# An encoder layer with three mixers: weight tiles split once and fetched as two parts, and an FFN input normalised ahead of its products

## The chip, the cores and the metric

The kernel runs on one core of a Trainium2 chip. The metric is the device time in microseconds of one execution of the whole program; the runs are compared by their median. Engine names are those of the profile: PE (TensorE matmul), PEld (its weight loads), DVE (VectorE), ACT (ScalarE), POOL (GpSimd), SP (SyncE, which here issues every DMA).

## The reference

One encoder layer over 2048 tokens of width 1024, in fp32:

```
h = rms_norm(x) * norm_mix;  p = h @ w_in          # 13 parts of p feed three mixers
out_a = sparse attention: an indexer scores all keys, each query keeps its 256 best, softmax over them
out_b = gated linear attention in chunks of 64;  out_c = sliding window attention with sinks
x = x + concat(out_a, out_b, out_c) @ w_out
h = rms_norm(x) * norm_ffn
x = x + (silu(h @ w_ffn_gate) * (h @ w_ffn_up)) @ w_ffn_down      # inner width 2816
return rms_norm(x) * final_norm
```

## The kernel before

**Layout.** Activations are kept transposed: a tile has 128 channels on the partitions and 512 tokens along the free side. The 2048 tokens are four groups of 512 (NG, G), the 1024 channels eight chunks (KC), the inner width 22 chunks (NF).

**Split products.** A product in fp32 is made of three matmuls in fp32r, of 512 columns each. Every operand is split in a part hi, rounded to fp32r, and a remainder lo. `split` (L113) does that with a cast on ACT (L116) and a subtraction on POOL (L119), and `product` (L150) and `proj` (L469) issue hi x hi, lo x hi and hi x lo for each chunk.

**Weights.** A weight tile is 128 x 512, which is four chunks of 128 x 128, 256 KB. Each use of a tile begins with `load_w` (L142 in the FFN, L459 in the projections): SP fetches it from DRAM to one of three buffers `raw`, and `split` fills a slot of `whi` and one of `wlo`. There are three such slots in the projections (A_W), five in the FFN of groups 0 and 1 (N_W), nine in the last FFN. The same tile of w_in is used for each of the four groups; the tiles of w_out and of the three FFN matrices are used three times, once for group 0, once for group 1 and once for groups 2 and 3 together, and each time fetched and split anew.

**Two threads.** `dense` (L1073) does `pass1` for the four groups (the parts of p that the sparse attention needs), then `pass2` (gated linear and window attention), then `ffn` for groups 0 and 1. `dsa` (L1058) does the sparse attention for 16 blocks of 128 queries: `select` (L825) searches the threshold of the 256 best by 31 halvings, each a count over all keys (on ACT at L888, on DVE at L890 in turn) and two DVE steps of one column (L913 and L915), while `attend` (L953) works on the block before. `merge` (L43) interleaves the two threads by the costs that they yield. A planner then puts the instructions in order for each engine: of those that it takes for ready, the earliest in the program goes first, and each engine runs its own in that order. An `ffn` begins with the attention's result for its groups (mixT in DRAM). When both threads are done, `ffn` runs for groups 2 and 3 (two halves of 512 tokens) by itself.

**The FFN** (L135). `mixed` (L186) fetches the mixers' output and splits it. For each output chunk oc and each half the w_out product is made, first over chunks 2 to 7 (`others`), then over 0 and 1 (`sparse`), which come from the sparse attention and are late; the first n_lead products go ahead without them. `residual` (L194) adds x and sums the squares. Then h2, x2 times the norm's weight but not yet times 1/rms, is split (L230, L231). For each f, `gate_up` (L234) makes the gate and the up product for each half; the factor 1/rms, `rs`, comes from a matmul with ones after the first gate product (`norm_scale`, L178), and is multiplied in behind the products:

```
V.tensor_mul(z, pg, rs[:, hs])       # L247: gate, from PSUM
Q.tensor_mul(u, z, rs[:, hs])        # L249
sigmoid(z, s)                        # L128 to L132: Abs, Exp, Ln, a DVE step, Exp
V.tensor_mul(u, pu, u)               # L254: up, from PSUM
Q.tensor_mul(u, u, s)                # L255
split(u, ah[:, hs], al[:, hs])
```

`down` (L259) multiplies two chunks f at a time by w_down and adds to x2 (L274). The last `down` also sums squares, and `finish` (L290) scales and stores the output. The sigmoid is written with Exp and Ln, as the norms are (`rstd_of`, L121), and one table is loaded on ACT at the start (L90).

Of the kernel before, what the change touches and what calls it, by code (L numbers as in the profile page):

```python
# [8 lines left out]
F32 = mybir.dt.float32  # L9
# [10 lines left out]
P = 128  # L20
# [64 lines left out]
def hybrid_encoder_kernel(ctx, tc, xT, w_in, w_out, w_g, w_u, w_d, vec, wuk, wuv, wg2,  # L85
# [27 lines left out]
    def split(src, hi, lo, hi_eng=None):  # L113
# [21 lines left out]
    def ffn(groups, pools, ps_f, ps_n, n_raw, n_w, n_act, n_lead, before):  # L135
# [3 lines left out]
        W = nh * 512  # L139
        halves = [slice(i * 512, (i + 1) * 512) for i in range(nh)]  # L140

        def load_w(src):  # L142
            raw = fr.tile([P, 512], F32, tag="raw", bufs=n_raw, name="raw")
            nc.sync.dma_start(out=raw, in_=src)
            hi = fh.tile([P, 512], F32R, tag="whi", bufs=n_w, name="whi")
            lo = fl.tile([P, 512], F32R, tag="wlo", bufs=n_w, name="wlo")
            split(raw, hi, lo)
            return hi, lo

        def product(ps, w, act, hs, ks=range(KC), first=True, last=True):  # L150
            for k in ks:
                hi, lo = w[k // 4]
                a, b = (t[:, (k % 4) * P:(k % 4 + 1) * P] for t in (hi, lo))
                T.matmul(ps, a, act[k][0][:, hs], start=(first and k == ks[0]), stop=False)  # L154
                T.matmul(ps, b, act[k][0][:, hs], start=False, stop=False)  # L155
                T.matmul(ps, a, act[k][1][:, hs], start=False, stop=(last and k == ks[-1]))  # L156
# [6 lines left out]
        def operand(k):  # L163
            pool = fo if k in others else fs
            return (pool.tile([P, W], F32R, tag=f"ah{k}", bufs=1, name="ah"),
                    pool.tile([P, W], F32R, tag=f"al{k}", bufs=1, name="al"))

        def square(hs, k):

# [11 lines left out]
            T.matmul(pm, ones, rs[:, hs], start=True, stop=True)  # L181
            rstd_of(pm, D, rs[:, hs])

        mixo = [operand(k) for k in range(KC)]

        def mixed(k):  # L186
            for g, hs in zip(groups, halves):
                hi, lo = (t[:, hs] for t in mixo[k])
                m = fr.tile([P, 512], F32, tag="m", bufs=3, name="m")
                nc.sync.dma_start(out=m, in_=mixT[g][k])  # L190
                A.copy(hi, m)
                (V if k % 2 else Q).tensor_sub(lo, m, hi.bitcast(F32))  # L192

        def residual(oc, i, ps):  # L194
            g, hs = groups[i], halves[i]
# [1 line left out]
            V.tensor_add(x2[:, oc, hs], x2[:, oc, hs], ps)  # L197
            square(hs, oc)

        for k in others:  # L200
            mixed(k)
            yield 0.5
        lead = []
        for oc in range(KC):
            w = [load_w(w_out[oc][:, i * 512:(i + 1) * 512]) for i in range(2)]
            for i, hs in enumerate(halves):
                ps = ps_f()
                yield from product(ps, w, mixo, hs, others, last=False)
                lead.append((oc, i, ps, w, hs))
                yield 3.9 - 0.65 * (KC - FINE)  # L210
                if oc * nh + i < n_lead - 1:
                    continue
                if oc * nh + i == n_lead - 1:
                    yield from before
                    rs = fx.tile([P, W], F32, tag="rs", bufs=1, name="rs")
                    x2 = fx.tile([P, KC, W], F32, tag="x2", bufs=1, name="x2")
                    for k in sparse:
                        mixed(k)
                while lead:
                    oc_, i_, ps, w_, hs_ = lead.pop(0)  # L220
                    yield from product(ps, w_, mixo, hs_, sparse, first=False)
                    residual(oc_, i_, ps)
                    yield 1.3

        h2 = [operand(k) for k in range(KC)]
        for hs in halves:
            for k in range(KC):
                gk = vc[:, V_FFN + k:V_FFN + k + 1]
                hi, lo = h2[k][0][:, hs], h2[k][1][:, hs]
                A.activation(hi, x2[:, k, hs], AF.Copy, scale=gk)  # L230
                V.scalar_tensor_tensor(out=lo, in0=x2[:, k, hs], scalar=gk, in1=hi.bitcast(F32),  # L231
                                       op0=ALU.mult, op1=ALU.subtract)

        def gate_up(f):  # L234
            ah = ft.tile([P, W], F32R, tag="fh", bufs=n_act, name="fh")
            al = ft.tile([P, W], F32R, tag="fl", bufs=n_act, name="fl")
            wg_ = [load_w(w_g[f][:, i * 512:(i + 1) * 512]) for i in range(2)]
            wu_ = [load_w(w_u[f][:, i * 512:(i + 1) * 512]) for i in range(2)]
            acts[f] = (ah, al)
            for i, hs in enumerate(halves):  # L240
                pg = ps_f()
                yield from product(pg, wg_, h2, hs)
                if f == 0:
                    norm_scale(hs)
                s = ft.tile([P, 512], F32, tag="s", bufs=2, name="s")
                z = ft.tile([P, 512], F32, tag="z", bufs=2, name="z")
                V.tensor_mul(z, pg, rs[:, hs])  # L247
                u = ft.tile([P, 512], F32, tag="u", bufs=2, name="u")
                Q.tensor_mul(u, z, rs[:, hs])  # L249
                sigmoid(z, s)  # L250
                yield 5.2 - 0.65 * (KC - FINE)
                pu = ps_f()
                yield from product(pu, wu_, h2, hs)
                V.tensor_mul(u, pu, u)  # L254
                Q.tensor_mul(u, u, s)  # L255
                split(u, ah[:, hs], al[:, hs])
                yield 5.2 - 0.65 * (KC - FINE)

        def down(fs, parts, last=False):  # L259

            n, ws = len(fs), {}
            for i2, hs in parts:
                if i2 not in ws:
                    ws[i2] = [load_w(w_d[f][:, i2 * 512:(i2 + 1) * 512]) for f in fs]
# [58 lines left out]
    with ExitStack() as mx:  # L323
# [132 lines left out]
                yield 0.4  # L456
            return hh, hl

        def load_w(src):  # L459
            raw = wp.tile([P, 512], F32, tag="raw", bufs=A_RAW, name="raw")  # L460
            nc.sync.dma_start(out=raw, in_=src)
            hi = wp.tile([P, 512], F32R, tag="whi", name="whi")
            lo = wp.tile([P, 512], F32R, tag="wlo", name="wlo")
            split(raw, hi, lo)
            return hi, lo

        PART = 0.65 * (KC - FINE)

        def proj(c, h, ws=()):  # L469
# [2 lines left out]
            ps = ps_mm()  # L472
            for k in range(KC):
                if k % 4 == 0:
                    hi, lo = ws[k // 4] if ws else load_w(w_in[c][:, k * P:k * P + 512])
# [7 lines left out]


        def pass1(g):
            ws = [load_w(w_in[CH_C][:, i * 512:(i + 1) * 512]) for i in range(2)]
            h, acc = yield from scaled_in(g)
            g0 = g * G

# [709 lines left out]
```

## Time and profile before

| | us |
|---|---|
| runs: median (lowest to highest) | 3005.09 (3005.06 to 3010.59) |
| the profiled execution: time | 3006.77 |
| the profiled execution: span in the trace | 3005.0 |
| PE / DVE / ACT / POOL busy | 2773.4 / 1803.9 / 1556.9 / 1372.3 |

The trace has one execution. Busy time of PE is to be read with care: matmuls overlap, each is shown as some 390 ns, and one can start every 226 ns. A share of busy time over the whole span is a mean over stages that differ; so the views below are cut by stage.

### The profile page before, as it was taken

The numbers are of one execution on the slowest core, as the hardware profiler recorded it, in microseconds if no ns is written. First come the engines' busy times: TensorE is split into PE (matmuls) and PEld (weight loads), VectorE is DVE, ScalarE is ACT, GpSimd is POOL, SyncE is SP. The second block draws the span as 40 slices with busy tenths as digits, with TensorE's granted clock in tenths as the row PEclk, the third lists the DMA queues.
The fourth block names the chain that finished last, engine by engine and source line by source line (L and its number), as shares of the span: only waits on it lengthen the run. The fifth ranks groups of instructions, "written<-read, shape, count | busy, mean of one in ns | idle before, by whom it ended". The sixth has DMA issues, their size and how long they took to land.

```text
span 3005.0 us, 38463 instructions
## 1 busy us (share of the span) xinstructions
PE 2773.4 (92%) x13364; PEld 2177.9 (72%) x13364; DVE 1803.9 (60%) x3638; ACT 1556.9 (52%) x2734; POOL 1372.3 (46%) x1085
## 2 busy tenths in 40 slices
PE   7688989999999989999989989999799999999997
PEld 5466757666676767777767777777588888888886
DVE  4588788786877867667577476575423223332226
ACT  4566666566565756565475464565525333223333
POOL 4334323333233345655654556546425445444543
PEclk9889999999999999999999999999999999999998
DMA  5444222122222322222223222222421111111111
GB/s 158 124 123 131 75 66 90 61 92 66 60 68 71 114 81 77 85 78 74 83 90 134 76 73 82 76 71 74 136 98 50 50 46 53 49 48 44 53 46 56
DMA packets 158874, 239.07 MB, mean 80 GB/s; under 512 B 16248, under 2 KB 56472, under 8 KB 158680
## 3 DMA queue, kind: packets, MB, share of 16 engines
q1 hardware_dynamic: 158680, 236.62, 25.2%
q8 instruction: 105, 1.72, 0.2%
q14 instruction: 89, 0.73, 0.1%
HBM read 212.83 MB, written 23.72 MB: 79 GB/s over the span
## 4 chain that ended last, share of the span: by engine, by line
PE 44%; DVE 10%; issue 5%; ACT 5%; POOL 4%; DMA 1%; DVEq 0%; SPq 0%; POOLq 0%; ACTq 0%
PE pf L154 6%; PE pf L156 6%; PE pf L155 6%; DVE jd L890 4%; PE mf L154 3%; PE mf L156 3%; PE mf L155 3%; PE pf L273 3%; PE pf L271 3%; PE pf L272 3%; POOL wlo L119 2%; ACT jd L888 2%; PE mf L271 2%; PE mf L273 2%; PE mf L272 1%
## 5 line engine op out<-in xcount | busy, mean ns | idle before, releaser
L119 POOL TENSOR_TENSOR wlo<-raw,whi 128x512 fp32r<-128x512 f32 x620 | 841.0, 1364 | 999.7 <-ACT whi L116 928.2
L116 ACT CAST whi<-raw 128x512 fp32r<-128x512 f32 x620 | 377.8, 616 | 420.7 <-PE pf L273 142.9
L888 ACT ACTIVATE jd<-x,c 128x384 bf16<-128x384 f32 (+13 forms) x224 | 292.6, 1306 | 191.1 <-DVE c L915 146.0
L154 PE MATMUL mf<-ah,whi 128*128 128x512 f32 x832 | 331.3, 398 | 13.3 <-ACT ah L230 10.9
L477 PE MATMUL mm<-hh,whi 128*128 128x512 f32 x704 | 297.9, 424 | 40.8 <-ACT hh L432 32.7
L890 DVE TENSOR_SCALAR_CACHE_REDUCE jd<-x,c 128x384 bf16<-128x384 f32 (+13 forms) x224 | 331.0, 1478 | 6.9
L156 PE MATMUL mf<-al,whi 128*128 128x512 f32 x832 | 327.9, 395 | 6.5 <-POOL al L192 3.5
L155 PE MATMUL mf<-ah,wlo 128*128 128x512 f32 x832 | 327.8, 395 | 0.9 <-POOL wlo L119 0.9
L154 PE MATMUL pf<-ah,whi 128*128 128x512 f32 x832 | 324.6, 390 | 1.0 <-issue 1.0
L155 PE MATMUL pf<-ah,wlo 128*128 128x512 f32 x832 | 323.7, 389 | 0.0
L156 PE MATMUL pf<-al,whi 128*128 128x512 f32 x832 | 323.6, 389 | 0.0
L479 PE MATMUL mm<-hl,whi 128*128 128x512 f32 x704 | 287.7, 412 | 7.1 <-DVE hl L433 6.0
L478 PE MATMUL mm<-hh,wlo 128*128 128x512 f32 x704 | 288.0, 410 | 2.7 <-POOL wlo L119 2.7
L477 PEld LDWEIGHTS mm<-hh,whi 128*128 128x128 f32 x704 | 138.4, 197 | 86.0 <-ACT hh L432 34.7
L154 PEld LDWEIGHTS mf<-ah,whi 128*128 128x128 f32 x832 | 158.2, 190 | 48.5 <-ACT ah L230 11.4
L156 PEld LDWEIGHTS mf<-al,whi 128*128 128x128 f32 x832 | 157.9, 190 | 41.8 <-POOL al L192 4.3
L274 DVE TENSOR_TENSOR x<-x,pf 128x512 f32<-128x512 f32 (+1 forms) x184 | 121.8, 664 | 109.4 <-PE pf L273 109.1
L155 PEld LDWEIGHTS mf<-ah,wlo 128*128 128x128 f32 x832 | 158.2, 190 | 34.2 <-POOL wlo L119 1.9
L271 PE MATMUL mf<-fh,whi 128*128 128x512 f32 x352 | 145.5, 413 | 39.8 <-DVE u L254 27.6
L154 PEld LDWEIGHTS pf<-ah,whi 128*128 128x128 f32 x832 | 156.2, 188 | 33.9 <-issue 1.5
L155 PEld LDWEIGHTS pf<-ah,wlo 128*128 128x128 f32 x832 | 156.2, 188 | 32.9 <-issue 0.5
L156 PEld LDWEIGHTS pf<-al,whi 128*128 128x128 f32 x832 | 156.1, 188 | 32.7 <-DVE al L231 0.2
(246 smaller groups left out, 5740.2 us busy)
## 6 DMA issues: line engine op xcount, KB each, us to landing
raw<-in_w_in_dram SPq DMA_DIRECT2D x176, 256.0 KB, 2.7
raw<-in_w_g_dram SPq DMA_DIRECT2D x132, 256.0 KB, 2.6
raw<-in_w_u_dram SPq DMA_DIRECT2D x132, 256.0 KB, 2.7
raw<-in_w_d_dram SPq DMA_DIRECT2D x132, 256.0 KB, 2.7
xk<-in_xT_dram SPq DMA_DIRECT2D x64, 256.0 KB, 2.9
raw<-in_w_out_dram SPq DMA_DIRECT2D x48, 256.0 KB, 3.0
m<-mixT SPq DMA_DIRECT2D x32, 256.0 KB, 3.3
x<-in_xT_dram SPq DMA_DIRECT2D x32, 256.0 KB, 4.5
```

The costliest lines, as they stand in the source:

```text
L116: A.copy(hi, src)
L119: Q.tensor_sub(lo, src, hi.bitcast(F32))
L154: T.matmul(ps, a, act[k][0][:, hs], start=(first and k == ks[0]), stop=False)
L155: T.matmul(ps, b, act[k][0][:, hs], start=False, stop=False)
L156: T.matmul(ps, a, act[k][1][:, hs], start=False, stop=(last and k == ks[-1]))
L271: T.matmul(ps, hi[:, os_], ah[:, hs], start=(j == 0), stop=False)
L273: T.matmul(ps, hi[:, os_], al[:, hs], start=False, stop=(j == n - 1))
L477: T.matmul(ps, a, hh[k], start=(k == 0), stop=False)
L478: T.matmul(ps, b, hh[k], start=False, stop=False)
L479: T.matmul(ps, a, hl[k], start=False, stop=(k == KC - 1))
L888: A.activation(jd, xs, AF.Sign, scale=-1.0, bias=c[:, 0:1], accum_out=cnt)
L890: V.tensor_scalar(out=jd, in0=xs, scalar1=c[:, 0:1], scalar2=0.0, op0=ALU.is_ge, op1=ALU.add, accum_out=cnt)
```

## The change

The change does three things.

1. `load_halves` and `store_halves` are new. A slot `w` has both parts of a weight tile, 128 x 1024. At the first use of a tile it is fetched and split as before and, two loads later, stored to DRAM in both parts (512 KB). At each later use both parts come from there with one DMA, straight to the slot, without `raw` and `split`. The numbers of slots and of raw buffers stay.
2. The FFN takes one half after the other in the w_out products (so the last FFN runs through w_out twice), fetches the second half's mixT tiles during the first half's last products, and `normed` makes h2 with 1/rms in it, per half, before the gate and up products.
3. The gate is pg * (1 + tanh(pg / 2)) / 2: one Tanh that reads PSUM, and two fused DVE steps, the second with the up product.

The diff, cut to its core (`mixed`, `operand` and `product` now take a half's own tiles instead of a slice; `proj`'s `load_w` calls `load_halves` in the same way with slots of `wp`):

```diff
+    halved, unstored = {}, []
+    def load_halves(key, src, raw_pool, n_raw, pool, n_w):
+        w = pool.tile([P, 1024], F32R, tag="w", bufs=n_w, name="w")
+        hi, lo = w[:, 0:512], w[:, 512:1024]
+        if key in halved:
+            while unstored:
+                store_halves()
+            nc.sync.dma_start(out=w.bitcast(F32), in_=halved[key])
+            return hi, lo
+        raw = raw_pool.tile([P, 512], F32, tag="raw", bufs=n_raw, name="raw")
+        nc.sync.dma_start(out=raw, in_=src)
+        split(raw, hi, lo)
+        halved[key] = dram.tile([P, 1024], F32, name=f"w{len(halved)}")
+        unstored.append((halved[key], w))
+        if len(unstored) > 2:
+            store_halves()
+        return hi, lo
+    def store_halves():
+        dst, w = unstored.pop(0)
+        nc.sync.dma_start(out=dst, in_=w.bitcast(F32))
...
-        def load_w(src):
...
+        def load_w(src, f, c):
+            return load_halves((src.tensor.name, f, c), src[f][:, c * 512:(c + 1) * 512], fr, n_raw, fh, n_w)
...
+        def normed(i):
+            hs = halves[i]
+            norm_scale(hs)
+            h2.append([])
+            for k in range(KC):
+                h2[i].append(operand(i, k))
+                hi, lo = h2[i][k]
+                hf = fr.tile([P, 512], F32, tag="m", bufs=3, name="hf")
+                V.scalar_tensor_tensor(out=hf, in0=x2[:, k, hs], scalar=vc[:, V_FFN + k:V_FFN + k + 1],
+                                       in1=rs[:, hs], op0=ALU.mult, op1=ALU.mult)
+                A.copy(hi, hf)
+                (V if k % 2 else Q).tensor_sub(lo, hf, hi.bitcast(F32))
+                yield 0.4
...
-        for oc in range(KC):
-            w = [load_w(w_out[oc][:, i * 512:(i + 1) * 512]) for i in range(2)]
-            for i, hs in enumerate(halves):
+        for i, hs in enumerate(halves):
+            lead = []
+            for oc in range(KC):
+                w = [load_w(w_out, oc, c) for c in range(2)]
...
+                if i + 1 < nh and oc >= n_lead:
+                    for k in range((oc - n_lead) * KC // (KC - n_lead), (oc + 1 - n_lead) * KC // (KC - n_lead)):
+                        mixed(i + 1, k)
...
-        h2 = [operand(k) for k in range(KC)]
-        for hs in halves:
-            for k in range(KC):
-                gk = vc[:, V_FFN + k:V_FFN + k + 1]
-                hi, lo = h2[k][0][:, hs], h2[k][1][:, hs]
-                A.activation(hi, x2[:, k, hs], AF.Copy, scale=gk)
-                V.scalar_tensor_tensor(out=lo, in0=x2[:, k, hs], scalar=gk, in1=hi.bitcast(F32),
-                                       op0=ALU.mult, op1=ALU.subtract)
+            yield from normed(i)
...
                 pg = ps_f()
-                yield from product(pg, wg_, h2, hs)
-                if f == 0:
-                    norm_scale(hs)
+                yield from product(pg, wg_, h2[i])
                 s = ft.tile([P, 512], F32, tag="s", bufs=2, name="s")
-                z = ft.tile([P, 512], F32, tag="z", bufs=2, name="z")
-                V.tensor_mul(z, pg, rs[:, hs])
-                u = ft.tile([P, 512], F32, tag="u", bufs=2, name="u")
-                Q.tensor_mul(u, z, rs[:, hs])
-                sigmoid(z, s)
+                A.activation(s, pg, AF.Tanh, scale=0.5)
+                V.scalar_tensor_tensor(out=s, in0=s, scalar=1.0, in1=pg, op0=ALU.add, op1=ALU.mult)
...
-                V.tensor_mul(u, pu, u)
-                Q.tensor_mul(u, u, s)
+                u = ft.tile([P, 512], F32, tag="u", bufs=2, name="u")
+                V.scalar_tensor_tensor(out=u, in0=s, scalar=0.5, in1=pu, op0=ALU.mult, op1=ALU.mult)
                 split(u, ah[:, hs], al[:, hs])
...
+            while unstored:
+                store_halves()
             dx.close()
```

## Rows read from the trace of the kernel before

**Rows 1.** Page, section 1: engine, busy us (share of the span), instructions.
```profile
PE 2773.4 (92%) x13364; PEld 2177.9 (72%) x13364; DVE 1803.9 (60%) x3638; ACT 1556.9 (52%) x2734; POOL 1372.3 (46%) x1085
```

**Rows 2.** Stages: window, length, busy us (instructions) per engine, granted clock, DMA share, GB/s.
```profile
0.00:1034.00 1034.00, 914.25 (x4607) 669.46 (x4608) 774.40 (x1925) 629.97 (x1268) 364.33 (x316) 0.94 0.30 91
1034.00:1572.00 538.00, 501.12 (x2455) 401.55 (x2454) 367.99 (x669) 319.30 (x506) 303.96 (x234) 0.98 0.27 84
1572.00:2120.00 548.00, 505.32 (x2425) 404.76 (x2424) 354.37 (x593) 306.03 (x467) 305.65 (x228) 0.97 0.25 82
2120.00:2176.00 56.00, 40.83 (x273) 29.75 (x272) 27.86 (x59) 32.33 (x53) 27.10 (x21) 0.88 0.50 163
2176.00:2960.00 784.00, 784.00 (x3456) 648.25 (x3455) 244.59 (x339) 246.57 (x398) 354.06 (x272) 1.00 0.16 53
```

**Rows 3.** The same view, 100 us in the middle of the last stage.
```profile
2300.00:2400.00 100.00, 100.00 (x443) 82.81 (x442) 27.08 (x37) 34.55 (x56) 53.87 (x42) 1.00 0.17 53
```

**Rows 4.** Groups: tile, shape, count | busy us, mean ns | idle before, releasers.
```profile
L119 POOL TENSOR_TENSOR wlo<-raw,whi 128x512 fp32r<-128x512 f32 x620 | 841.0, 1364 | 999.7 <-ACT whi L116 928.2 <-issue 46.7 <-PE mm L478 7.0
L116 ACT CAST whi<-raw 128x512 fp32r<-128x512 f32 x620 | 377.8, 616 | 420.7 <-PE pf L273 142.9 <-PE pf L156 92.7 <-PE mf L156 71.2
L154 PE MATMUL mf<-ah,whi 128*128 128x512 f32 x832 | 331.3, 398 | 13.3 <-ACT ah L230 10.9 <-DVE x L274 1.3 <-ACT ah L191 0.9
...
L478 PE MATMUL mm<-hh,wlo 128*128 128x512 f32 x704 | 288.0, 410 | 2.7 <-POOL wlo L119 2.7
...
L271 PE MATMUL mf<-fh,whi 128*128 128x512 f32 x352 | 145.5, 413 | 39.8 <-DVE u L254 27.6 <-DVE x L274 10.3 <-ACT fh L116 1.7
...
L249 POOL TENSOR_TENSOR u<-z,rs 128x512 f32<-128x512 f32 x88 | 122.5, 1393 | 59.6 <-DVE z L247 56.3 <-DMA raw<-in_w_d_dram 2.3 <-DVE e L904 1.0
...
L255 POOL TENSOR_TENSOR u<-u,s 128x512 f32<-128x512 f32 x88 | 116.8, 1327 | 121.7 <-DVE u L254 101.9 <-ACT s L132 13.0 <-ACT whi L116 6.9
...
L130 ACT ACTIVATE s<-s 128x512 f32<-128x512 f32 x88 | 55.6, 631 | 2.1
...
L231 DVE SCALAR_TENSOR_TENSOR al<-x,vc,ah 128x512 fp32r<-128x512 f32 x32 | 24.9, 828 | 0.6 <-ACT ah L230 0.5
...
L230 ACT ACTIVATE ah<-x,vc 128x512 fp32r<-128x512 f32 x32 | 20.8, 711 | 4.5 <-PE pf L155 4.5
```

**Rows 5.** Chain of waits, shares of the window: 1034 to 1572, then 1572 to 2120.
```profile
by line: issue 13.5%; DVE jd L890 9.2%; PE mf L154 7.8%; PE mf L155 7.4%; PE mf L156 7.4%; ACT jd L888 5.2%; POOL wlo L119 4.5%; PE mf L271 4.2%; PE mf L273 4.1%; PE mf L272 4.0%; PE o L1011 2.1%; POOL u L255 1.6%; DVE up L913 1.6%; ACT big
...
by line: issue 14.3%; DVE jd L890 11.0%; PE mf L156 7.2%; PE mf L154 7.2%; PE mf L155 7.1%; POOL wlo L119 5.4%; PE mf L271 4.5%; PE mf L273 4.3%; PE mf L272 4.2%; ACT jd L888 4.2%; POOL u L255 2.2%; PE o L1011 1.7%; DVE up L913 1.6%; DVE c 
```

**Rows 6.** Stages, the instructions of line 119 alone.
```profile
0.00:1034.00 1034.00, 260.57 (x191) 0.94 0.30 91
```

**Rows 7.** DMA issues: count, KB each, median us from issue to landing.
```profile
raw<-in_w_in_dram SPq DMA_DIRECT2D x176, 256.0 KB, 2.7
...
out_dram<-x SPq DMA_DIRECT2D x12, 512.0 KB, 3.1
...
out_dram<-x SPq DMA_DIRECT2D x8, 256.0 KB, 2.4
```

**Rows 8.** Waits of the SP queue, 0 to 1034: us in total, times, longest.
```profile
SPq L461 <- POOL wlo L119: 450.4, 150, 10.5
SPq L710 <- POOL mixb L706: 58.3, 16, 15.0
SPq L785 <- ACT mc L784: 55.8, 14, 12.4
SPq L976 <- DVE least L988: 43.9, 17, 10.0
```

**Rows 9.** Line 131: duration ns min/median/max, first and last start.
```profile
L131 DVE SCALAR_TENSOR_TENSOR s<-z,s x88: 678/1072/1801, 1102.1 to 2936.8; 128x512 f32<-128x512 f32 x88
```

**Rows 10.** Timeline of the start: start us, us, instruction.
```profile
0.74 1.28 ACT L90 ACT_TABLE_LOAD   x1 [0.74 <-PEq L1188]
```

**Rows 11.** Line 181, columns as in rows 9.
```profile
L181 PE MATMUL tr<-rs,ones x8: 590/594/697, 1096.4 to 2122.8; 128*128 128x512 f32 x8
```

More of the change, by code (lines that the diff above doesn't have):

```diff
@@ L140, in ffn, with product @@
         halves = [slice(i * 512, (i + 1) * 512) for i in range(nh)]
-        def load_w(src):
[L143 to L150, printed above, removed]
+        def load_w(src, f, c):
+            return load_halves((src.tensor.name, f, c), src[f][:, c * 512:(c + 1) * 512], fr, n_raw, fh, n_w)
+        def product(ps, w, act, ks=range(KC), first=True, last=True):
             for k in ks:
@@ L153, in product @@
                 a, b = (t[:, (k % 4) * P:(k % 4 + 1) * P] for t in (hi, lo))
-                T.matmul(ps, a, act[k][0][:, hs], start=(first and k == ks[0]), stop=False)
-                T.matmul(ps, b, act[k][0][:, hs], start=False, stop=False)
-                T.matmul(ps, a, act[k][1][:, hs], start=False, stop=(last and k == ks[-1]))
+                T.matmul(ps, a, act[k][0], start=(first and k == ks[0]), stop=False)
+                T.matmul(ps, b, act[k][0], start=False, stop=False)
+                T.matmul(ps, a, act[k][1], start=False, stop=(last and k == ks[-1]))
                 if k % FINE == FINE - 1 and k < ks[-1]:
@@ L182, in norm_scale, with mixed @@
             rstd_of(pm, D, rs[:, hs])
[L184 to L192, printed above, removed]
+        mixo = [[operand(i, k) for k in range(KC)] for i in range(nh)]
+        def mixed(i, k):
+            hi, lo = mixo[i][k]
+            m = fr.tile([P, 512], F32, tag="m", bufs=3, name="m")
+            nc.sync.dma_start(out=m, in_=mixT[groups[i]][k])
+            A.copy(hi, m)
+            (V if k % 2 else Q).tensor_sub(lo, m, hi.bitcast(F32))
         def residual(oc, i, ps):
@@ L198, in residual @@
             square(hs, oc)
-        for k in others:
-            mixed(k)
-            yield 0.5
-        lead = []
-        for oc in range(KC):
-            w = [load_w(w_out[oc][:, i * 512:(i + 1) * 512]) for i in range(2)]
-            for i, hs in enumerate(halves):
+        def normed(i):
[11 more added lines that the diff above has]
+                yield 0.4
+        for k in others:
+            mixed(0, k)
+            yield 0.25
+        h2 = []
+        rs = x2 = None
+        for i, hs in enumerate(halves):
+            lead = []
+            for oc in range(KC):
+                w = [load_w(w_out, oc, c) for c in range(2)]
                 ps = ps_f()
-                yield from product(ps, w, mixo, hs, others, last=False)
-                lead.append((oc, i, ps, w, hs))
+                yield from product(ps, w, mixo[i], others, last=False)
+                lead.append((oc, ps, w))
                 yield 3.9 - 0.65 * (KC - FINE)
-                if oc * nh + i < n_lead - 1:
+                if i == 0 and oc < n_lead - 1:
                     continue
-                if oc * nh + i == n_lead - 1:
+                if i == 0 and oc == n_lead - 1:
                     yield from before
@@ L217, in ffn @@
                     for k in sparse:
-                        mixed(k)
+                        mixed(0, k)
+                if i + 1 < nh and oc >= n_lead:
+                    for k in range((oc - n_lead) * KC // (KC - n_lead), (oc + 1 - n_lead) * KC // (KC - n_lead)):
+                        mixed(i + 1, k)
                 while lead:
-                    oc_, i_, ps, w_, hs_ = lead.pop(0)
-                    yield from product(ps, w_, mixo, hs_, sparse, first=False)
-                    residual(oc_, i_, ps)
+                    oc_, ps, w_ = lead.pop(0)
+                    yield from product(ps, w_, mixo[i], sparse, first=False)
+                    residual(oc_, i, ps)
                     yield 1.3
-        h2 = [operand(k) for k in range(KC)]
-        for hs in halves:
-            for k in range(KC):
-                gk = vc[:, V_FFN + k:V_FFN + k + 1]
-                hi, lo = h2[k][0][:, hs], h2[k][1][:, hs]
-                A.activation(hi, x2[:, k, hs], AF.Copy, scale=gk)
-                V.scalar_tensor_tensor(out=lo, in0=x2[:, k, hs], scalar=gk, in1=hi.bitcast(F32),
-                                       op0=ALU.mult, op1=ALU.subtract)
+            yield from normed(i)
         def gate_up(f):
@@ L263, in down @@
                 if i2 not in ws:
-                    ws[i2] = [load_w(w_d[f][:, i2 * 512:(i2 + 1) * 512]) for f in fs]
+                    ws[i2] = [load_w(w_d, f, i2) for f in fs]
                 for oc in range(i2 * 4, i2 * 4 + 4):
@@ L457, in norm_in, with load_w @@
             return hh, hl
[L459 to L465, printed above, removed]
+        def load_w(c, i):
+            return load_halves(("in", c, i), w_in[c][:, i * 512:(i + 1) * 512], wp, A_RAW, wp, A_W)
         PART = 0.65 * (KC - FINE)
@@ L474, in proj @@
                 if k % 4 == 0:
-                    hi, lo = ws[k // 4] if ws else load_w(w_in[c][:, k * P:k * P + 512])
+                    hi, lo = ws[k // 4] if ws else load_w(c, k // 4)
                 a, b = hi[:, (k % 4) * P:(k % 4 + 1) * P], lo[:, (k % 4) * P:(k % 4 + 1) * P]
@@ L485, in pass1 @@
         def pass1(g):
-            ws = [load_w(w_in[CH_C][:, i * 512:(i + 1) * 512]) for i in range(2)]
+            ws = [load_w(CH_C, i) for i in range(2)]
             h, acc = yield from scaled_in(g)
```

12 lines of the change are left out of this document (6 added, 6 removed).

## The prediction

> **What bounds the kernel now.** I read the stages first [rows 1, 2]. Cut at the points where the work changes hands, the span has four parts: A, 0 to 1034 us, the projections beside the sparse attention; B, 1034 to 2120, the FFN of token groups 0 and 1 beside the rest of the sparse attention; a short end of the last attention block, to 2176; and C, the FFN of groups 2 and 3 alone. The reader is to see that C stands at 784.00 us of PE busy in 784, at granted clock 1.00, with ACT and POOL under half used. A steady stretch of C shows what that is worth: 443 products in 100 us, 226 ns each [rows 3]. Nothing that ACT, DVE or POOL are spared can shorten C; only its start and its end are open. So the question is what A and B do.
>
> In A and B the PE is busy by the page, but not full. In A there are 704 x 3 projection products, 477 us at 226 ns; in B 3 x 832 + 3 x 352 = 3552 products of both groups, 803 us of a stage of 1086 [rows 4]. What keeps the rest of the time is a lockstep with the attention's search, whose steps alternate between ACT and DVE: on the chain of waits of B the search's lines jd and up hold 16 to 17% and the matmuls in the list about 37%, but POOL's weight remainder wlo also stands there with 4.5 and 5.4%, and POOL's u with 1.6 and 2.2% [rows 5]. That chain is the measure of what the change can give back in B. In A the DVE is the fullest engine after PE: 774 us of 1034 [rows 2].
>
> **Weight tiles.** The kernel converts 620 tiles: on ACT a cast of 616 ns, on POOL a subtraction of 1364 ns [rows 4]. After the change a tile is converted at its first use only: 44 of w_in's 176, 16 of w_out, 132 of the three FFN matrices (44 each), 192 in all. C now runs w_out once per half, so there are 636 tile uses, of which 444 become plain fetches. Removed: 428 x 0.616 = 264 us of ACT and 428 x 1.364 = 584 us of POOL. By place: A loses 132 of 176 (81 us ACT, and 180 us of the 261 that POOL spends there on wlo [rows 6]); group 0's FFN loses none, since it is the first user; group 1's loses all 148 (91 and 202 us); C keeps none, and gains nothing by it.
>
> What it adds: 192 stores and 444 fetches of 512 KB where there were fetches of 256 KB. No row shows a 512 KB fetch. The nearest are the 256 KB weight fetch at 2.7 us and the output stores, 2.4 us for 256 KB and 3.1 us for 512 KB [rows 7]; 2.7 + 0.7 = 3.4 us is my value, 2.7 and 5.4 (twice) the ends. Bytes: group 0's FFN is the heaviest place, 148 tiles of 0.26 MB read and 0.52 MB written in 538 us, 216 GB/s instead of its 84 at a share of 0.27 [rows 2]; in proportion the share becomes 0.7. That is room, with longer landings.
>
> A fetch now lands in the slot that the PE reads, and can only be issued when that slot's last product is done. In A there are three slots, so the SP queue has two tiles' time: on the mean 2 x 1034/176 = 11.8 us, at the tightest 2 x 12 x 0.226 = 5.4 us. 3.4 us fit in both. Before, three raw buffers stood ahead of the slots, and SP was already waiting for them (450.4 us on wlo in A [rows 8]); a store waits for the same subtraction that the next raw load waited for, so on first uses it delays little. What is queued behind a waiting fetch is what was queued behind a waiting raw load: the attention's near, qa and qf loads and the mixT stores. Cost 0, with the far end kept as a rival.
>
> **What the freed engines are worth in A and B.** The same DVE operation s, always 128 x 512 with both operands in SBUF, takes 678 ns at best, 1072 at the median and 1801 at worst [rows 9]; I put the spread down to POOL's products that run beside it. With half of A's POOL work gone I count 40 us less of DVE's 774, an estimate; the chain shows only the last 100 us of A, so between 0 and 87 us (these 40, and half of ACT's 81 with a few us for wlo) I take half of the DVE part: **A -20 us**. In B the lines that vanish from the chain are wlo in group 1, 5.4% of 548 = 30 us, and u, 1.6% of 538 and 2.2% of 548 = 21 us [rows 5]: 51 us, and as much again at most in lines below the list (the cast, the old gate's steps). When a piece goes, the search step or the product next to it is late instead, so half of the 102 stays: **B -50 us**, between 0 and -102.
>
> **The gate.** Per f and half, ACT drops Abs, Exp, Ln, Exp (4 x 0.631) for one Tanh, POOL drops two products (1.39 and 1.33), and DVE has two fused operations where it had three [rows 4]. In B that is 44 x 1.9 = 83 us of ACT and 44 x 2.7 = 120 us of POOL; their worth is in the B term, since the rows u are this. The gate's PSUM bank is held longer, by Tanh and a second operation instead of one: some 0.6 us against a 5.4 us product, hidden by it. In C all of it is hidden behind the PE.
>
> No row shows a Tanh. The trace has one table load on ACT, 1.28 us at the start [rows 10], although Ln, Exp, Abs, Square and Sign alternate all through: one table holds these. Whether it holds Tanh is not to be seen; the price is between 0 and one load for each change of function, and I take the low part: two loads around each norm that stands alone. The Trainium skill, page "ScalarE: Activation LUTs", section "Table sets: the hidden batching unit", lists tanh with exp in one set, and exp with ln in another, without tanh. By that rule it is the norm's Ln, not the search or the attention's Exp, that changes tables, up to 16 times for the eight norms after the first Tanh; at the trace's 1.28 us 20 us, at the page's 2.66 us 43 us, most of it beside the PE.
>
> **The norm ahead of the products.** Before, the FFN's first product waited only for the scaled copy ah (10.9 us of idle PE in all [rows 4]). Now it waits for the sum's matmul (0.59 us [rows 11]), Ln and Exp (0.63 each), a DVE product (0.83, as the old al) and a cast (0.62), in place of one scaled copy (0.71) [rows 4]: 2.6 us and some hops, 3.2 us, at each of the two starts in B; two loads at group 1's norm and two at the last one make 5.1. In C the first half's norm is covered by the second half's w_out products, the second's by two products of the first half (10.8 us); and only half of the mixT tiles has to be there before C's first product. **+12 us**, between 0 and +30.
>
> **Sum.** The profiled execution took 3006.8 us, 1.8 around its span of 3005.0; -20 -50 +12 = -58 gives 2949, and the median of the runs lies 1.7 lower: **2947 us**.
>
> **Rivals.**
> Everything goes: A -87 and B -102 without a next wait, norm at +12: 2828 at the far end; 2866 with four fifths of the gain. For it: DVE and ACT are shared by both threads. Against: the search's own steps, which are untouched, are the chain's biggest part.
> Hidden anyway: the search and the PE set the order, and what POOL and ACT drop was beside them; 0 to -15 with +12 for the norm: 3000.
> The other side: a fetch that starts too late. SP stands in A for 58.3, 55.8 and 43.9 us behind stores and loads that wait for POOL, ACT and DVE, up to 15.0 us at once [rows 8], and the weights behind them are only two tiles ahead now instead of six. If two thirds of these 158 us reach the PE, A grows by 105 and the rest of the sum holds: 3052. It decides from the point where waits on SP and landing together exceed the 5.4 to 11.8 us. Against: the mean wait is 3.4 us (158 in 47), and the trace before shows the PE waiting for wlo 2.7 us in all of A [rows 4].
> The tables change at every Tanh beside the attention: 44 Tanh in B, two loads each, 88 x 1.28 = 113 us of ACT in the lockstep, half or all exposed: 3003 to 3060. Against it stands the sentence on the skill above.
> That a fetch would not replace the conversion I see no way for.
>
> **Chances.** Forecast (2900 to 2985) 0.52; everything goes 0.14; hidden 0.14; late fetch 0.15; tables 0.05. Range 2860 to 3030: it leaves out the far ends of the first and the last two. This kernel's runs tell 0.2%, 6 us, from no change. Faster: 0.52 + 0.14 + 0.09 of the hidden case = 0.75; within 0.2%: 0.05; slower: 0.20.
>
> **What would show it.** wlo and whi at 192 each and POOL's busy time down by some 820 us (584, and 88 x 2.7 of the gate); PE in C still 443 per 100 us; C's length within 10 us of 829; group 1's FFN shorter than group 0's; DVE's s-like operations nearer 0.69 us; PE not waiting for a fetched w. Wrong: mm products waiting for DMA w in A; table loads in the tens; or A and B as long as before with POOL half empty.

## The result, and the profile after

The changed kernel takes 2974.07 us in the median (2969.60 to 2981.09, 4 runs) against 3006.04 before (3005.06 to 3010.59, 4 runs). The ratio is 0.9893, with 95% interval [0.9869, 0.9916]: 32 us less, where 58 were forecast. The total lies inside the range, but not by the forecast's steps. The profiled execution has a span of 2969.7 us, at a granted clock of 0.969 over the whole.

I cut every kernel below at starts of products on the PE. A ends where group 0's first FFN product starts (tile mf). The next cuts are the start of group 1's first, of the last mf product, and of C's first (tile pf).

| profiled execution | A | group 0's FFN | group 1's | attention's end | C |
|---|---|---|---|---|---|
| before | 1030.3 | 539.0 | 550.5 | 56.0 | 829.3 |
| after | 997.4 | 549.0 | 542.3 | 41.6 | 839.4 |
| difference | -32.9 | +10.0 | -8.2 | -14.4 | +10.1 |

Only A moved as forecast. B as I had defined it did not get shorter (1089.5, 1091.3); the attention's end did, which I had left out; C got longer.

The page after, section 1, to be read against [rows 1]: POOL fell by 791 us (820 forecast), ACT by 376, DVE by 119, and PE's work is the same.

```profile
PE 2760.8 (93%) x13364; PEld 2169.2 (73%) x13364; DVE 1684.5 (57%) x3566; ACT 1181.0 (40%) x2059; POOL 581.7 (20%) x497
```

The stages of the changed kernel, with the columns of [rows 2]:

```profile
0.00:997.00 997.00, 892.02 (x4587) 657.49 (x4587) 723.70 (x1914) 557.27 (x1130) 178.12 (x182) 0.95 0.48 152
997.00:1546.00 549.00, 514.34 (x2472) 410.83 (x2473) 359.21 (x670) 285.23 (x443) 246.93 (x191) 0.97 0.65 225
1546.00:2089.00 543.00, 505.18 (x2440) 404.03 (x2440) 325.65 (x573) 196.09 (x263) 52.61 (x46) 0.97 0.46 153
2089.00:2130.00 41.00, 34.41 (x258) 24.23 (x256) 24.57 (x51) 25.31 (x37) 11.06 (x8) 1.00 0.63 226
2130.00:2925.00 795.00, 790.23 (x3473) 651.27 (x3474) 217.98 (x309) 87.42 (x139) 75.98 (x57) 1.00 0.33 111
```

The third row is the one to look at: in group 1's FFN POOL has gone from 306 us of work to 53 and ACT from 306 to 196 [rows 2], and the stage is 8 us shorter. In A the column to follow is DVE: 51 us less for nearly the same number of instructions (1914; 1925 before), while A lost 33. The row of before in [rows 2] reaches 4 us past A's end; with both cut at A's end, DVE has 47 us less (771.50 and 724.10).

The middle of C, as in [rows 3]: 443 products in 100 us again.

```profile
2300.00:2400.00 100.00, 100.00 (x443) 82.78 (x442) 28.90 (x42) 6.72 (x11) 7.75 (x6) 1.00 0.28 95
```

Groups after, as in [rows 4]: 192 conversions, as counted, at the same price each; the Tanh, which no row of before showed, takes 0.60 us, and its table loads come on top. Two more loads stand outside the two rows of them: at the first Tanh (L277) and at an Exp of the attention (L1015).

```profile
L119 POOL TENSOR_TENSOR w<-raw,w 128x512 fp32r<-128x512 f32 x192 | 259.8, 1361 | 340.2 <-ACT w L116 312.4 <-issue 8.0 <-PE mf L177 4.7
L116 ACT CAST w<-raw 128x512 fp32r<-128x512 f32 x192 | 116.9, 616 | 108.3 <-PE mf L177 34.8 <-PE mf L301 12.7 <-issue 12.2
L299 PE MATMUL mf<-fh,w 128*128 128x512 f32 x352 | 147.7, 420 | 28.2 <-DVE x L302 12.7 <-DVE u L283 11.1 <-ACT fh L116 2.8
L277 ACT ACTIVATE s<-mf 128x512 f32<-128x512 f32 x44 | 26.0, 590 | 57.3 <-PE mf L177 57.3
L148 ACT ACT_TABLE_LOAD x8 | 10.3, 1283 | 0.1
L149 ACT ACT_TABLE_LOAD x7 | 9.0, 1283 | 0.1
```

DMA issues after, as in [rows 7], and the SP queue's waits in A, as in [rows 8]: a 512 KB fetch or store lands in 3.5 us in the median (3.4 was the estimate); the raw fetches that are left take 3.7 where they took 2.7. SP no longer waits 450 us for POOL, but 237 us for the PE to free a slot.

```profile
w<-w SPq DMA_DIRECT2D x636, 512.0 KB, 3.5
...
raw<-in_w_in_dram SPq DMA_DIRECT2D x44, 256.0 KB, 3.7
```

```profile
SPq L131 <- PE mm L502: 237.5, 81, 10.1
SPq L144 <- POOL w L119: 87.0, 39, 5.8
...
SPq L808 <- ACT mc L807: 49.1, 14, 11.9
SPq L733 <- POOL mixb L729: 46.0, 14, 8.5
```

The chain of waits in group 1's FFN after, as the second line of [rows 5]: POOL's wlo (5.4%) and u (2.2%) are gone from it. Their place is taken by the search's steps on ACT (4.2% before, 10.0% now) and DVE (11.0%, now 12.6%), and by the products. The share called issue, in which the profile shows no wait, fell as well, from 14.3 to 4.6%.

```profile
by line: DVE jd L913 12.6%; PE mf L177 10.0%; ACT jd L911 10.0%; PE mf L176 9.7%; PE mf L175 9.7%; issue 4.6%; PE mf L301 4.2%; PE mf L299 4.1%; PE mf L300 4.1%; DVE c L938 2.2%; DVE up L936 2.2%; DVE x L302 1.9%; PE o L1034 1.8%; PE tr L10
```

### The profile page after: what moved, and what is told of

The parts are those of the page before. It is cut to its first block, busy times and chain, and to the rows that moved or that the text cites. A ratio compares the mean times of both kernels' runs of the same rounds, so it can differ in the third digit from the quotient of the medians.

```text
span 2969.7 us, 36770 instructions
## 1 busy us (share of the span) xinstructions
PE 2760.8 (93%) x13364; PEld 2169.2 (73%) x13364; DVE 1684.5 (57%) x3566; ACT 1181.0 (40%) x2059; POOL 581.7 (20%) x497
## 5 line engine op out<-in xcount | busy, mean ns | idle before, releaser
L500 PE MATMUL mm<-hh,w 128*128 128x512 f32 x704 | 297.1, 423 | 51.3 <-ACT hh L460 45.0
L177 PE MATMUL mf<-al,w 128*128 128x512 f32 x832 | 327.0, 394 | 10.5 <-POOL al L232 4.5
L175 PE MATMUL mf<-ah,w 128*128 128x512 f32 x832 | 328.6, 395 | 0.4 <-DVE ro L725 0.4
L175 PE MATMUL pf<-ah,w 128*128 128x512 f32 x832 | 324.1, 390 | 2.7 <-ACT ah L211 1.0
L119 POOL TENSOR_TENSOR w<-raw,w 128x512 fp32r<-128x512 f32 x192 | 259.8, 1361 | 340.2 <-ACT w L116 312.4
L176 PE MATMUL mf<-ah,w 128*128 128x512 f32 x832 | 325.8, 393 | 0.4 <-POOL w L119 0.3
L177 PE MATMUL pf<-al,w 128*128 128x512 f32 x832 | 324.0, 389 | 1.4 <-POOL al L212 0.6
L176 PE MATMUL pf<-ah,w 128*128 128x512 f32 x832 | 324.5, 390 | 0.0
L502 PE MATMUL mm<-hl,w 128*128 128x512 f32 x704 | 286.6, 410 | 6.1 <-POOL hl L483 3.3
L501 PE MATMUL mm<-hh,w 128*128 128x512 f32 x704 | 286.7, 408 | 2.1 <-POOL w L119 2.1
L177 PEld LDWEIGHTS mf<-al,w 128*128 128x128 f32 x832 | 157.2, 189 | 47.7 <-POOL al L232 6.5
L175 PEld LDWEIGHTS pf<-ah,w 128*128 128x128 f32 x832 | 156.2, 188 | 36.3 <-ACT ah L211 1.9
L175 PEld LDWEIGHTS mf<-ah,w 128*128 128x128 f32 x832 | 157.6, 189 | 33.6 <-issue 0.9
L176 PEld LDWEIGHTS mf<-ah,w 128*128 128x128 f32 x832 | 157.4, 189 | 33.3 <-POOL w L119 1.5
L176 PEld LDWEIGHTS pf<-ah,w 128*128 128x128 f32 x832 | 156.2, 188 | 32.8 <-issue 0.5
```

The lines of the kernel that those rows point to most:

```text
L175: T.matmul(ps, a, act[k][0], start=(first and k == ks[0]), stop=False)
L176: T.matmul(ps, b, act[k][0], start=False, stop=False)
L177: T.matmul(ps, a, act[k][1], start=False, stop=(last and k == ks[-1]))
```

## The experiments

Each kernel was timed in 3 rounds against the kernel before on the same chip. "B+" is the time from group 0's first FFN product to C's first, the attention's end included, since both threads end there. The stages come from one profiled execution of each kernel. Kernels in which the code of A is the same as after (e5_two, e6_sign, e8_order) show an A of 997.4 to 1002.5, and after and e8_order, with the same B, a B+ of 1132.9 and 1136.9. So differences of some 5 us in a stage are not told apart.

| kernel | median us | ratio to before, 95% | A | B+ | C |
|---|---|---|---|---|---|
| before | 3006.04 | | 1030.3 | 1145.4 | 829.3 |
| after | 2974.07 | 0.9893 [0.9869, 0.9916] | 997.4 | 1132.9 | 839.4 |
| e1_weights | 2957.73 | 0.9841 [0.9817, 0.9865] | 995.6 | 1127.2 | 828.9 |
| e2_ffn | 3012.41 | 1.0014 [0.9999, 1.0028] | 1029.6 | 1134.9 | 843.1 |
| e3_nostore | 2962.25 | 0.9851 [0.9831, 0.9872] | 991.7 | 1130.3 | 838.0 |
| e4_ready | 2957.73 | 0.9840 [0.9819, 0.9860] | 986.5 | 1132.8 | 841.0 |
| e5_two | 2826.47 | 0.9406 [0.9389, 0.9422] | 998.6 | 984.2 | 842.6 |
| e6_sign | 2971.93 | 0.9889 [0.9870, 0.9909] | 998.2 | 1137.3 | 833.7 |
| e8_order | 2981.03 | 0.9916 [0.9898, 0.9934] | 1002.5 | 1136.9 | 847.4 |
| e9_pool | 3048.29 | 1.0156 [1.0134, 1.0178] | 1089.7 | 1128.4 | 828.9 |
| e12_pool2 | 2990.95 | 0.9946 [0.9931, 0.9961] | 1031.3 | 1128.2 | 828.9 |
| e14_bias | 2947.47 | 0.9809 [0.9789, 0.9829] | 985.6 | 1130.8 | 828.9 |
| e15_bias_speed | 2992.37 | 0.9945 [0.9921, 0.9969] | 1034.3 | 1117.6 | 832.9 |
| e16_bias_slow | 3021.75 | 1.0065 [1.0042, 1.0088] | 982.7 | 1206.3 | 828.9 |

**The two parts alone.** e1_weights puts the stored halves into the kernel before; e2_ffn takes them out of the changed one.

```diff
 e1: kernel before
-            w = [load_w(w_out[oc][:, i * 512:(i + 1) * 512]) for i in range(2)]
+            w = [load_w(w_out, oc, i) for i in range(2)]     # and so for w_in, w_g, w_u, w_d
 e2: changed kernel
-        halved[key] = dram.tile([P, 1024], F32, name=f"w{len(halved)}")
-        unstored.append((halved[key], w))
-        if len(unstored) > 2:
-            store_halves()
```

> The kernel before with the weight change alone (its old FFN: unscaled norm, old gate, w_out once for both halves of C). Cut at the first product of each stage, the kernel before has A 1030, group 0's FFN 539, group 1's 550, end of the attention 56, C 829; the changed kernel 997, 549, 542, 42, 839. Theory (the relief of POOL and ACT is worth A and nothing in B, and the new FFN costs C its 10): A 990 to 1005, the two FFN beside the attention together 1082 to 1095, C 829, in all about 2965. Rival (B did gain some 50 from the weights and lost them again to the new norm and its table loads): B 1045 or less with the old norm, in all 2925 or less. Second rival (the gain in A comes from the new FFN's planning): A 1025 to 1035, in all about 3005.

> The changed kernel, but every use of a weight tile fetches 256 KB and converts it, as before: the new FFN alone. Theory: A 1028 to 1033, the two FFN beside the attention 1085 to 1095 although ACT and POOL are spared some 200 us of the old gate there, C about 839: in all 3005 to 3020. Rival (the gate's relief is worth something in B): B 1065 or less, in all 2985 or less.

The weights alone give 48 us, 16 more than the whole change, and the intervals of the two ratios don't meet. The new FFN alone is no gain: its ratio's interval reaches from no change to 0.3% slower, with A as before and C 14 us longer. The theory on e2 held in each stage. So all of A's gain belongs to the weights and all of C's loss to the FFN. B+ is where both theories on e1 missed: it fell by 18, neither by nothing nor by 50. And the parts don't add: -18 for the weights, -10 for the FFN, -12 for both.

**What the stores and conversions cost.** Both kernels fetch each later use from one of the first eight stored tiles (so with the wrong weights); e3_nostore still converts each first use, e4_ready only those eight.

```diff
+            nc.sync.dma_start(out=w.bitcast(F32), in_=stored[halved[key] % 8])
 ...
+        if len(stored) < 8:
+            stored.append(dram.tile([P, 1024], F32, name=f"w{len(stored)}"))
+            nc.sync.dma_start(out=stored[-1], in_=w.bitcast(F32))
 e4, besides:
+        if len(stored) == 8:
+            halved.setdefault(key, len(halved))
```

> The changed kernel without 184 of its 192 stores: the first eight tiles are stored, and each later use fetches one of these eight (other weights than it should, the same 512 KB). First uses convert as in the changed kernel. Theory (the stores cost group 0's FFN and the start of A some us, and nothing hides behind them): group 0's FFN 549 to about 540, A 997 to 990, in all 2955 to 2970. Rival (the stores ate B's gain): group 0's FFN 515 or less, in all 2940 or less.

> As the run without stores, but beyond the first eight tiles no tile is converted at all: every other use fetches 512 KB of one of the eight (other weights than it should). It takes the last 184 conversions away too, 113 us of ACT and 251 us of POOL, 148 of them in group 0's FFN. Theory (B is held by the products and their lockstep with the attention): group 0's FFN 530 to 545, B 1070 to 1090, A 980 to 995, in all 2940 to 2960. Rival (conversions are worth time in B, about the 5 % that wlo held on the chain): group 0's FFN 510 or less, in all 2930 or less.

184 stores are worth 12 us in the medians (the two intervals just meet), of which by the stages A shows 6 and B+ 3. Without the last 184 conversions, 251 us of POOL, A is 5 us shorter, no more than equal kernels differ by, and B+ is not shorter (1130.3, 1132.8); the totals don't tell these two kernels apart. The rival of an eaten gain falls: no gain of the size of B's 50 us lies under the stores.

**What holds B.** In groups 0 and 1, gate and up leave out one product of three, and so lose precision.

```diff
-                T.matmul(ps, b, act[k][0], start=False, stop=False)
+                if nh > 1 or len(ks) < KC:
+                    T.matmul(ps, b, act[k][0], start=False, stop=False)
```

> The changed kernel, in which gate and up of groups 0 and 1 leave out the product of the weights' remainder: two products of three, 704 fewer at 0.226, 159 us of PE work out of B (and the values are no longer exact). Theory (in B the PE's products are the limit, the search's lockstep and the engines beside it are not): group 0's FFN to the start of C, 1133 us in the changed kernel, falls by 120 to 159, in all 2815 to 2855. Rival (the search's lockstep between ACT and DVE holds B): it falls by less than 60, in all 2915 or more.

B+ falls by 148.7 of the 159 us that were taken from the PE. The trace says the same in another way. Give each PE instruction of B+ the usual distance of its shape to the next one, taken near the fast end of what is seen: the PE's work is then some 936 us in the kernel before, 938 after and 936 in e1_weights, and its starts lose 210, 195 and 191 us beyond that. The split depends on what is called usual, since the attention's small products have no steady distance: at the median distance the work is some 1015 us in each and the loss 130, 117 and 111. By either count POOL and ACT could only have given back a part of that loss, and they gave 14 to 19.

**The table loads.** Sign stands in the place of Tanh (another gate, so other values).

```diff
-                A.activation(s, pg, AF.Tanh, scale=0.5)
+                A.activation(s, pg, AF.Sign, scale=0.5)
```

> The changed kernel with Sign in the place of Tanh (another gate, so other values): Sign runs from the table that is loaded at the start, and the 17 later table loads go, 22 us of ACT. Theory (only loads on the PE's path count: some 6 us in the last norm and 2 to 3 at C's start): C 839 to 829 to 833, B as it was, in all 2960 to 2968. Rival (the loads also hold the lockstep in B): B and the attention's end together shorter by over 10 us, in all 2955 or less.

The 17 later loads are gone. C is 5.7 us shorter, the low end of what was expected, and B+ 4.4 longer, which is no more than equal kernels differ by; the medians, 2 us apart, tell no difference. Both totals missed. The rival, loads that hold B, falls.

**The order of w_out in C.** C takes each w_out tile for both halves at once again, and both norms after the last.

```diff
+            for oc in range(KC):
+                w = [load_w(w_out, oc, c) for c in range(2)]
+                for i, hs in enumerate(halves):
 ...
+            for i in range(nh):
+                yield from normed(i)
```

> The changed kernel with w_out in C in the order of before (each weight tile for both halves at once, both norms after the last). Theory (C's ten us are the mixT tiles that the first half's products run ahead of, about 4 us, the second half's norm with nothing of that half beside it, 2 us, and table loads): the two norms now come together with no product beside them, so C gets longer, 845 to 855, in all 2980 to 2990. Rival (the order by halves is what costs C its ten us): C 829 to 834, in all 2962 to 2968.

C 847.4, as the theory said: the order by halves doesn't cost C its ten us but by this stage saves 8, one norm being hidden behind the other half's products (the totals, 7 us apart, have intervals that meet). What C lost in the changed kernel are starts of products: by the first count above 17.3 us up to its last product, 9.0 before. With both norms at once it is the norm's operands that come late; the PE's waits of e8_order at C's start (2139 to 2270; us, times, longest):

```profile
PE pf L175 <- ACT ah L231: 4.5, 2, 3.3
PE pm L202 <- DMA w<-w: 2.6, 1, 2.6
PE pf L177 <- DVE al L232: 2.2, 3, 1.5
```

**Why A got shorter.** Two tries give POOL its subtractions in A back, with nobody reading the result.

```diff
 e9: e1_weights, at each fetch of a w_in tile
+                spare = raw_pool.tile([P, 512], F32, tag="raw", bufs=n_raw, name="raw")
+                Q.tensor_sub(spare..., one, one)          # one: ones, broadcast
 e12: the same place
+                spare = pool.tile([P, 512], F32, tag="spare", bufs=1, name="spare")
+                Q.tensor_sub(spare, lo.bitcast(F32), hi.bitcast(F32))
```

> The run with the weight change alone, and beside every fetch of a w_in tile POOL does a subtraction of the same size that nothing waits for (132 of them): POOL's load in A is again that of before. Theory of the prediction (A gains because POOL's products slow DVE's): A goes back from 996 by 20 us or more, to 1016 to 1030. Rival (A gains because weights no longer pass through a raw buffer, ACT and POOL on their way to the PE): A stays at 996 to 1004.

e9_pool (A 1089.7, where neither theory had it) tells nothing on the question. Its subtractions wait for no data, so POOL ran them in one bunch at 440 to 550 us with the projections' own hl behind them; the chain of waits from 430 to 590 holds them with 45%, and A lost far more than there was to lose:

```profile
by line: POOL raw L135 45.4%; issue 7.2%; DVE hf L476 6.6%; DVE jd L909 3.6%; DVE e L923 3.3%; POOL hl L479 3.1%; PE mm L498 2.8%; ACT jd L907 2.6%; POOL w L119 2.5%; PE mm L496 2.2%; PE mm L497 2.2%; POOL near L996 2.1%; PE ot L712 1.9%; P
```

> The weight change alone, and POOL again subtracts the two halves of every w_in tile that is fetched (132 times 128x512), into a spare tile that nothing reads. Each subtraction waits for its own fetch, so they are spread as the tiles come, not bunched as in the first try. Theory of the prediction (A gains because POOL's subtractions run beside DVE's products and slow them): A goes back from 996 by 15 to 34 us, to 1011 to 1030, and DVE's mean per product of two SBUF operands rises. Rival (A gains because the weights no longer pass through raw buffer, ACT and POOL on their way to the PE, and SP is freed): A stays at 994 to 1003.

With each subtraction tied to its own fetch, A is 1031.3, where it was 1030.3 before the change: the whole gain is gone. The weights still reach the PE by a plain fetch there, and ACT still has no casts for them, so neither the shorter path nor ACT's relief shows as a gain in A. A rival is that a subtraction holds the weight slot which it reads. In all of A the SP queue waits 1.1 us for these subtractions and the PE 1.9 us for a fetched w; but on the chain of waits the fetches of w hold 17 us, where e1_weights has none, so a smaller part of the 36 may have come by that way. The stages of A, first without and then with the 132 subtractions:

```profile
0.00:996.00 996.00, 888.77 (x4591) 655.73 (x4592) 727.25 (x1919) 559.56 (x1133) 177.59 (x182) 0.96 0.49 153
```

```profile
0.00:1031.00 1031.00, 899.20 (x4589) 659.01 (x4589) 764.47 (x1917) 558.46 (x1132) 354.64 (x314) 0.95 0.47 148
```

ACT and the DMA share stay, PE's busy time grows by 10; DVE's 1917 instructions take 37 us more, and the stage takes 35.7 more. Two DVE lines, 0 to 985 us, show 11 of the 37: first e1_weights, then e12_pool2 (columns: line, tiles, shape, count, busy us, mean ns).

```profile
L874 DVE SCALAR_TENSOR_TENSOR x<-r,w_tok,x 128x512 f32<-128x512 f32 x30 | 26.2, 875 | 4.3 <-ACT r L873 3.2
L780 DVE TENSOR_SCALAR l<-l,den 128x256 f32<-128x256 f32 x60 | 21.6, 413 | 0.3
```

```profile
L877 DVE SCALAR_TENSOR_TENSOR x<-r,w_tok,x 128x512 f32<-128x512 f32 x30 | 32.8, 1094 | 3.6 <-ACT r L876 2.4
L783 DVE TENSOR_SCALAR l<-l,den 128x256 f32<-128x256 f32 x55 | 25.8, 523 | 0.3
```

**The bias table and the planner's factor.** On e1_weights, the broadcast write of the bias table goes to ACT's queue, and the loads that read it for the sliding window come a group later; then the planner's factor is changed.

```diff
-            nc.sync.dma_start(out=bD.rearrange("h (q m) -> h q m", m=PITCH),
+            A.dma_start(out=bD.rearrange("h (q m) -> h q m", m=PITCH),
 ...
+                if g == 1:
+                    bias_swa()
 e15: SPEED = 1.4; e16: SPEED = 1.2
```

> The weight change alone, and the broadcast write of the bias table (bD, 1.5 MB) is issued from ACT's queue; the four loads that read it for the sliding-window attention come one group later, so SP doesn't stand 14 us for its landing. All parts are computed. Theory (both kernels with stored halves lose 15 us at the start because two xk tiles land behind bD's write, 34 us for two): the 192nd projection product comes at 95 to 100 us instead of 113, A 980 to 988, in all 2938 to 2946. Rival (the write takes the DMA engines whichever queue issues it, or the loss is given back within A): A 992 to 1000, in all 2950 to 2960.

> The run with the bias table moved, and the sparse attention planned as 1.4 instead of 1.3 times its cost, so that it runs ahead of the projections and the FFN and ends sooner. Theory (the attention's end, 55 us with the PE two thirds busy, is idle time that other work can fill): the end 55 to 35 or less, B longer by less, in all 5 to 15 below the run with the bias table moved alone. Rival (what the end loses, B gains, since both threads share the lockstep): within 4 us of that run.

> The weight change alone with the bias table moved, and the sparse attention planned at 1.2 times its cost instead of 1.3. At 1.4 A grew by 49 us, and B with its end fell by 13. Theory (the two stages trade against each other the same way on both sides): A 986 to 955 or less, B with its end 1131 to 1140 to 1150, in all 2925 to 2940. Rival (what A loses is work of the attention that B then has to carry beside the same products): B with its end grows by as much as A falls, in all 2945 to 2965.

e14_bias is the fastest kernel here, 2947.47 us, though its ratio's interval meets that of e1_weights, so the 10 us between the medians are not secured. The step I gave for it is wrong: the 192nd projection product still comes at 115 us (113 in e1_weights). The PE's wait behind the xk tiles (28 us) has gone, and a wait behind the attention's near loads, which read the same table and so wait for its landing, stands in its place; 10 us appear only after product 384. The lag at the start is made up later anyway: in the kernel before, the 192nd product comes at 94.8 us, 18 earlier than in e1_weights, but by the 384th e1_weights is only 3 us behind (193.6 and 196.4). The PE's and then the SP queue's longest wait, 60 to 120 us:

```profile
PE sc L1001 <- DVE least L1005: 26.3, 1, 26.3
```

```profile
SPq L993 <- DMA bD<-bt: 32.2, 1, 32.2
```

The planner's factor fell out against me on both sides. At 1.4 A grows by 49 and B+ falls by 13; at 1.2 A falls by 3 only, and the attention's end alone takes 141 us. Of these two runs neither theory nor rival held.

## Why the prediction was right or wrong

The sign and the range held, and A's step with them; B's step failed. That the total came into the range is in part luck: A gave 13 us more than its term, B's 50 did not come, and 14 came from the attention's end, which had no term.

*A -20.* The mechanism held, the size was small: -33. e12_pool2 takes all of it back with POOL's subtractions, and DVE's busy time grows by as much (+37 of DVE, +36 of A). I had counted 40 us of DVE and halved them. Both were low: DVE had 47 us less, and 33 of them, not half, came back. (The 261 us that I gave to wlo in A are all of line 119 there, 191 instructions, of which w_in's tiles are 176; that changes no term.) The Trainium skill, page "GPSIMD Engine Reference", section "Specifications", says that GpSimd shares its SBUF interfaces with VectorE and contends with DVE instructions in a 2-port perf mode or with two SBUF inputs. The first of the two lines above agrees: two tensor inputs in SBUF, 875 to 1094 ns. The second, a tensor-scalar, went from 413 to 523; whether it runs in such a mode no run shows.

*B -50.* This is the step that failed. I took the shares that wlo and u hold on the chain of waits as time that would come back, and as much again below the list. With five sixths of POOL's work gone from group 1's FFN (306 to 53 us) the chain ran through other lines, the stage was 8 us shorter, and group 0's, which converts as before and stores besides, 10 longer. With its end, B+ gained 12. The bound was in the trace: 936 to 1015 of 1145 us are the PE's work at its usual pace, and e5_two shows that B+ follows this work. The PE's waits there that name POOL came to 5 us, while wlo stood on the chain with 4.5 and 5.4% [rows 5]:

```profile
PE mf L271 <- DVE u L254: 27.6, 11, 5.8
...
PE mf L156 <- POOL al L192: 3.5, 2, 3.0
...
PE mf L155 <- POOL wlo L119: 0.9, 2, 0.5
...
PE mf L273 <- POOL fl L119: 0.4, 1, 0.4
```

"Hidden anyway" was the rival that described B.

*Left out: the attention's end.* I gave it no term, since no edit touched it. It took 14 us less after and 11 less in e2_ffn, but 1 less in e1_weights, where B took 17 less. Two threads share one planner, and only the sum B+ means anything. Why the two parts don't add in it, the runs leave open.

*Norm and tables +12.* A loss of about that size came, but in another place, so the number is right by luck. I put all but two table loads into B and took the norm in C for covered; C took 10 more. The table loads are 5.7 of these by e6_sign's C; the norm's operands are in the rest. In B the starts cost next to nothing: the PE waits for the norm's ah and al there came to 13 us before and 15 after with the norm's matmul.

*The table loads.* There are 17 after the start: one at the first Tanh and 16 around the eight norms. This agrees to the last load with the rule that the prediction took from the Trainium skill, page "ScalarE: Activation LUTs", section "Table sets: the hidden batching unit". Each load costs the 1.28 us of its own instruction. In C's second norm the Exp starts 0.01 us after its load ends:

```profile
2226.78 1.28 ACT L149 ACT_TABLE_LOAD   x1
2228.07 0.63 ACT L149 ACTIVATE rs<-rs 128x512 f32<-128x512 f32 x1
```

The 2.66 us that the Trainium skill gives for a switch (the same page, section "What ACT_TABLE_LOAD costs") are not seen here. The rival "tables at every Tanh" falls with the count.

*Fetch cost 0, and the late fetch.* Held: landing 3.5 us, DMA share 0.65 in group 0's FFN (0.7 estimated). SP waits 237 us for slots, but the PE's waits for a fetched tile are no line of its list in A. The stores, costed at nothing, took about 12 in the medians (e3_nostore), with intervals that just meet.

*What was to show it.* wlo at 192, 443 products in C's middle, and group 1's FFN shorter than group 0's came, the last of them more because group 0's FFN got longer. C's length stands just outside its 10 us. DVE's s operation, with the old gate in e1_weights, has a median of 693 ns where it had 1072 [rows 9].

## What to carry to other kernels

A share of the chain of waits says which work is late last, not what comes back without it: first see how much of the stage the limiting engine could lose at its usual pace (130 to 210 of 1145 us here), and what its own waits name. Work on POOL can be dear beside a busy DVE even where nobody waits for its result. Measure the two halves of a change apart: here the FFN half took back a third of what the weight half gave.

## What the runs showed of the hardware that I had not expected

132 POOL subtractions that nobody reads (1.34 us each, 177 us) cost 36 us of A (33 in the medians), while DVE's busy time rose by 37. And two 256 KB loads issued beside the broadcast write of the 1.5 MB bias table took 34 us on the chain of e1_weights (start, us), where the median of their kind there is 3.5:

```profile
59.95 34.10 DMA xk<-in_xT_dram x2
```
